# Decay masks from differences of cumulative sums: the broadcast through memory, the subtraction on GpSimd

## The chip, the cores and the metric

The kernel runs on one core of a Trainium2 chip. The metric is the device time of one execution in microseconds (us), median of several runs. The engines are named as the profile names them: PE (TensorE, matmul), DVE (VectorE), ACT (ScalarE), POOL (GpSimd) and SP (SyncE, which only issues DMAs here). Each engine works off its own list of instructions in a fixed order; one that waits for another engine holds up all behind it.

## The reference

A trunk of two layers over a sequence of 256 positions and 2048 features: first a gated delta rule mixer with a convolutional feed-forward block, then a differential attention with another such block. All is float32. The change concerns the mixer's decays alone. Per head (16 of them) the reference has a gate `g` for each position and uses, inside the chunks and between them, exponentials of differences of its cumulative sums:

```python
g = -jnp.exp(a_log) * jax.nn.softplus(a + dt_bias)
...
g = jnp.cumsum(to_chunks(g), axis=-1)
...
decay = jnp.exp(jnp.where(causal, g[..., :, None] - g[..., None, :], -jnp.inf))
...
lower = jnp.where(strict, jnp.einsum('bnhid,bnhjd->bnhij', kb, k) * decay, 0.0)
...
a_intra = jnp.where(causal, jnp.einsum('bnhid,bnhjd->bnhij', q, k) * decay, 0.0)
```

The kernel does not cut the sequence into four chunks. It treats it as two halves of 128 positions, and builds for each head a decay matrix `exp(G_i - G_j)`, zero where i < j, with j on the partitions: one of 128x256 (j in the first half, i in the whole sequence) in the tiles `ma1`, and one of 128x128 (both in the second half) in `ma2`.

## The kernel before

**The weight stream.** Nearly all time goes to products of weights with 2048 features. `wstat` makes one output tile of 128 columns: two transfers of 512 KB bring the weights (`raw`), ACT rounds them to a high part (`hi`, L206), DVE subtracts to get the low part (`lo`, L207), and PE does 16 matmuls with the high part (L228, 128x512) and 16 with the low part (L231, 128x256), all into one PSUM buffer. There are four such buffers (`ps_...`), four each of `raw`, `hi` and `lo`, so a tile's matmuls can't start before the buffer of the tile four places earlier has been read. `add_halves` (L253 and on) reads it: ACT copies one half to a buffer `c_...` (L258; two such buffers exist, tag `c256`), DVE adds the other (L259, which frees the PSUM buffer) and scales by the norm (L261).

**The first layer's opening.** The first three tiles stream together (`ps_in`): the gates (`ba`), the keys of head 0 (`s16`) and its queries (`s0`). Then for each further head a k tile and a q tile follow: k1, q1, k2, q2 and so on. `conv_silu` does the causal convolution of each (ACT L594, DVE L596 three times) and the SiLU (ACT L597, `kq`). `gates_and_decays` is written ahead of the loop over heads. It computes the gates on 16 partitions (L617 to L640, mostly DVE, with an exponential and a logarithm on ACT), transposes them by PE (`bgT_ps`, L644), and builds the decay matrices into the second half of `ma1` and `ma2`. `products` (L567 and on) then makes per head the products of keys with keys and queries on PE (`p1`, `p2`), transposes the queries (L577, squared on ACT, L579, `jq`) and multiplies by the decays on DVE (L583 to L586). The PSUM pool of these small products, `ax`, has four buffers as well.

**What sets the order.** The lists of PE, DVE, ACT and POOL are ordered by a scheduler that simulates the program while it is built; only SP's DMA issues are in the order written. So a change in `gates_and_decays` can move instructions of the k and q tiles around it.

**The decays before.** For four heads at a time DVE multiplies a triangular mask (`upto`) by the gates (L656, 128x512, twice), PE multiplies these by a second mask (`after`) or by ones (L661, L663, L665: `d1`, `d2`, `d3`, fp32, 128x512), which gives the differences of the sums at once in PSUM; DVE copies a column (L667, `sfx`), ACT takes exponentials out of PSUM (L670, L671, and L674 once per head with `sfx` as bias), and POOL zeroes what lies above the diagonal (L676).

Of the kernel before, what the change touches and what calls it, by code (L numbers as in the profile page):

```python
# [8 lines left out]
F32 = mybir.dt.float32  # L9
BF16 = mybir.dt.bfloat16  # L10
F32R = mybir.dt.float32r
AF = mybir.ActivationFunctionType
ALU = mybir.AluOpType
AX = mybir.AxisListType

P = 128
D = 2048
S = 256
KD = D // P
NH = 16  # L20
# [70 lines left out]
class Trunk:  # L91
# [507 lines left out]
    def gates_and_decays(self, ps, ma1, ma2, szt):  # L599
        nc = self.nc  # L600
        s = self.t([P, S], "ba_s", "s256")
        self.add_halves(s[0:64], ps, "ba", slice(0, 64))

        after, upto = szt[0][:, 1024:1152], szt[0][:, 1152:1280]
        nc.gpsimd.affine_select(
            out=after, in_=self.ones, compare_op=ALU.is_gt, fill=0.0,
            base=0, pattern=[[-1, P]], channel_multiplier=1,
        )
        nc.gpsimd.affine_select(
            out=upto, in_=self.ones, compare_op=ALU.is_ge, fill=0.0,  # L610
            base=0, pattern=[[1, P]], channel_multiplier=-1,
# [33 lines left out]
        bgT = self.cst.tile([P, 2, 64], F32, name="bgT")  # L645
        nc.vector.tensor_copy(bgT, pt[:, 0:128].rearrange("p (a c) -> p a c", a=2))


        sfx = self.t([P, NH], "sfx", "sfx", bufs=1)
        for q in range(4):  # L650
            hs = slice(q * 4, (q + 1) * 4)
            gm = []
            for p in range(2):
                o = (q % 2) * 1024 + p * 512
                m = szt[1][:, o:o + 512].rearrange("p (h i) -> p h i", h=4)
                nc.vector.tensor_tensor(  # L656
                    m, upto.unsqueeze(1).to_broadcast([P, 4, P]),
                    bgT[:, p, 32 + q * 4:36 + q * 4].unsqueeze(2).to_broadcast([P, 4, P]), op=ALU.mult)
                gm.append(m)
            d1 = self.ax(f"d1_{q}")  # L660
            nc.tensor.matmul(d1, after, gm[0], start=True, stop=True)  # L661
            d2 = self.ax(f"d2_{q}")
            nc.tensor.matmul(d2, after, gm[1], start=True, stop=True)  # L663
            d3 = self.ax(f"d3_{q}")
            nc.tensor.matmul(d3, self.ones, gm[1], start=True, stop=True)  # L665
            v = lambda x: x.rearrange("p (h i) -> p h i", h=4)
            nc.vector.tensor_copy(sfx[:, hs], v(d1)[:, :, P - 1])  # L667
            m1 = ma1[q].rearrange("p (h a i) -> p h a i", h=4, a=2)[:, :, 1, :]
            m2 = ma2[q // 2].rearrange("p (h a i) -> p h a i", h=8, a=2)[:, (q % 2) * 4:(q % 2) * 4 + 4, 1, :]
            nc.scalar.activation(m1[:, :, 0:P], v(d1), AF.Exp)  # L670
            nc.scalar.activation(m2, v(d2), AF.Exp)  # L671
            for j in range(4):
                h = q * 4 + j
                nc.scalar.activation(m1[:, j, P:S], d3[:, j * P:(j + 1) * P], AF.Exp, bias=sfx[:, h:h + 1])  # L674
            for m in (m1[:, :, 0:P], m2):
                nc.gpsimd.affine_select(out=m, in_=m, compare_op=ALU.is_ge, fill=0.0, base=0, pattern=[[0, 4], [1, P]], channel_multiplier=-1)  # L676
        return bgT[:, :, 0:NH]
# [354 lines left out]
```

## Time and profile before

| | us |
|---|---|
| three runs | 2451.94, 2445.16, 2448.11 |
| median | 2448.11 |
| the profiled execution | 2448.15 |
| its span on the core | 2446.4 |
| PE busy | 2412.2 (99% of the span) |
| DVE busy | 1665.8 (68%) |
| ACT busy | 1194.4 (49%) |
| POOL busy | 115.6 (5%) |
| mean granted clock of PE | 0.993 |

Read it by stage: the shares are means over a span in which nearly all is the weight stream. Times in the trace are from the span's start. The decays belong to the first 100 us: the three first tiles end at about 32, tile k2 starts at 42.65, the gates are done at 68.10, and the d matmuls run between 77.71 and 95.5.

### The profile page before, as it was taken

What the parts mean: (1) busy time and instruction counts of PE and PEld (TensorE: products, weight loads), DVE (VectorE), ACT (ScalarE), POOL (GpSimd) and SP (SyncE); (2) the same over time, 40 slices, a digit from 0 to 9 for tenths busy, and PEclk for the clock granted to TensorE, in tenths of its full rate; (3) what the DMA queues carried; (4) which work ended last, traced back from release to release, by engine and by line L of the source; (5) the groups of instructions that cost most, each with busy time, mean ns of one, the idle gap of its engine ahead of it and who ended that gap; (6) DMA issues with size and microseconds to landing.
All of it is one profiled execution on the core that took longest, in us unless ns stands there. A gap on an engine that the chain in (4) does not pass through costs nothing.

```text
span 2446.4 us, 35043 instructions
## 1 busy us (share of the span) xinstructions
PE 2412.2 (99%) x13211; PEld 2062.6 (84%) x13211; DVE 1665.8 (68%) x2603; ACT 1194.4 (49%) x1956; POOL 115.6 (5%) x185
## 2 busy tenths in 40 slices
PE   9999989999999999999999999999999999999998
PEld 7788868878888888888888888888888888888887
DVE  6888647857877777764446677556777777774444
ACT  6655424545544444444346555445544444444342
POOL 0100730100000000000000000000000000000000
PEclk9999989999999999999999999999999999999999
DMA  6365543444555555565554554455555555555554
GB/s 225 105 201 167 198 142 118 163 160 159 198 189 189 190 189 190 189 207 192 196 192 156 188 188 164 171 187 175 183 189 189 189 190 189 190 195 202 196 193 153
DMA packets 134730, 443.19 MB, mean 181 GB/s; under 512 B 26144, under 2 KB 26400, under 8 KB 134048
## 3 DMA queue, kind: packets, MB, share of 16 engines
q1 hardware_dynamic: 134560, 440.95, 52.9%
q8 instruction: 103, 1.69, 0.3%
q14 instruction: 67, 0.55, 0.1%
HBM read 437.21 MB, written 3.69 MB: 180 GB/s over the span
## 4 chain that ended last, share of the span: by engine, by line
PE 94%; POOL 2%; DVE 1%; ACT 1%; DMA 1%; issue 1%; SPq 0%; DVEq 0%; POOLq 0%; ACTq 0%
PE ps_up L228 26%; PE ps_up L231 13%; PE ps_d L299 7%; PE ps_d L298 7%; PE ps_d L297 7%; PE ps_v L228 3%; PE ps_ak L228 2%; PE ps_aq L228 2%; PE ps_k L228 2%; PE ps_q L228 2%; PE ps_v L231 1%; PE ps_wo L298 1%; PE ps_wo L299 1%; PE ps_av L297 1%; PE ps_av L299 1%; PE ps_av L298 1%
## 5 line engine op out<-in xcount | busy, mean ns | idle before, releaser
L228 PE MATMUL ps_up<-xT_f,hi_up 128*128 128x512 f32 x2752 | 865.7, 396 | 0.0
L231 PEld LDWEIGHTS ps_up<-xT_f,lo_up 128*128 128x128 f32 x2752 | 517.0, 188 | 121.1 <-DVE lo_up L207 0.6
L206 ACT CAST hi_up<-raw_up 128x1024 fp32r<-128x1024 f32 x344 | 360.6, 1050 | 477.7 <-issue 321.0
L207 DVE TENSOR_TENSOR lo_up<-raw_up,hi_up 128x1024 fp32r<-128x1024 f32 x344 | 421.4, 1225 | 198.3 <-ACT hi_up L206 197.9
L231 PE MATMUL ps_up<-xT_f,lo_up 128*128 128x256 f32 x2752 | 541.2, 278 | 0.0
L228 PEld LDWEIGHTS ps_up<-xT_f,hi_up 128*128 128x128 f32 x2752 | 419.3, 189 | 0.2
L207 DVE TENSOR_TENSOR lo_d<-raw_d,hi_d 128x1024 fp32r<-128x1024 f32 x168 | 205.8, 1225 | 224.3 <-ACT hi_d L206 224.3
L206 ACT CAST hi_d<-raw_d 128x1024 fp32r<-128x1024 f32 x168 | 177.0, 1053 | 256.7 <-PE ps_d L299 239.7
L299 PE MATMUL ps_d<-hi_d,hT 128*128 128x512 f32 x672 | 261.8, 390 | 0.0
L298 PE MATMUL ps_d<-lo_d,hT 128*128 128x512 f32 x672 | 261.8, 390 | 0.0
L297 PE MATMUL ps_d<-hi_d,hT 128*128 128x512 f32 x672 | 261.8, 390 | 0.0
L298 PEld LDWEIGHTS ps_d<-lo_d,hT 128*128 128x128 f32 x672 | 126.2, 188 | 26.2
L297 PEld LDWEIGHTS ps_d<-hi_d,hT 128*128 128x128 f32 x672 | 126.2, 188 | 26.2
L299 PEld LDWEIGHTS ps_d<-hi_d,hT 128*128 128x128 f32 x672 | 126.2, 188 | 25.9
L228 PE MATMUL ps_z<-xT_in,hi_z 128*128 128x512 f32 x256 | 82.8, 405 | 9.6 <-ACT hi_z L206 9.6
L228 PE MATMUL ps_v<-xT_in,hi_v 128*128 128x512 f32 x256 | 88.8, 421 | 1.8 <-ACT hi_v L206 1.8
L828 DVE SCALAR_TENSOR_TENSOR gy<-gs,c_fconv,gy 128x255 f32<-128x255 f32 (+1 forms) x176 | 84.3, 480 | 2.9
L228 PE MATMUL ps_ak<-xT_kv,hi_ak 128*128 128x512 f32 x240 | 79.5, 408 | 0.0
L228 PE MATMUL ps_k<-xT_in,hi_k 128*128 128x512 f32 x240 | 77.9, 405 | 1.1 <-DVE s L259 1.1
L228 PE MATMUL ps_q<-xT_in,hi_q 128*128 128x512 f32 x240 | 76.6, 399 | 1.4 <-DVE s L259 1.4
L174 POOL TENSOR_SCALAR qr<-q 128x1 f32<-128x1 f32 x8 | 1.5, 191 | 1584.5 <-DVE q L424 1584.5
L596 DVE SCALAR_TENSOR_TENSOR y<-s,c_gconv,y 128x255 f32<-128x255 f32 (+1 forms) x144 | 68.2, 484 | 9.3 <-ACT y L594 7.6
(382 smaller groups left out, 3890.2 us busy)
## 6 DMA issues: line engine op xcount, KB each, us to landing
raw_up<-in_w_up SPq DMA_DIRECT2D x344, 512.0 KB, 4.3
raw_d<-in_w_dn SPq DMA_DIRECT2D x176, 512.0 KB, 3.3
raw_z<-in_w_in SPq DMA_DIRECT2D x32, 512.0 KB, 3.3
raw_v<-in_w_in SPq DMA_DIRECT2D x32, 512.0 KB, 3.3
raw_wo<-in_w_out SPq DMA_DIRECT2D x32, 512.0 KB, 3.3
raw_av<-in_w_v SPq DMA_DIRECT2D x32, 512.0 KB, 3.2
raw_ao<-in_w_o SPq DMA_DIRECT2D x32, 512.0 KB, 3.3
raw_k<-in_w_in SPq DMA_DIRECT2D x30, 512.0 KB, 3.3
```

The lines of the kernel that those rows point to most:

```text
L174: nc.gpsimd.tensor_scalar(dst, src, scale, EPS, op0=ALU.mult, op1=ALU.add)
L206: nc.scalar.copy(hi[:, c], raw[:, c])
L207: nc.vector.tensor_tensor(lo[:, c], raw[:, c], hi[:, c].bitcast(F32), op=ALU.subtract)
L228: nc.tensor.matmul(to, parts[i][0][:, k % 8 * P:(k % 8 + 1) * P], x, start=(k == 0 and tt != 1), stop=False)
L231: nc.tensor.matmul(ps[i][:, 256:512], parts[i][1][:, k % 8 * P:(k % 8 + 1) * P], xT.hi(k), start=False, stop=(k == KD - 1))
L297: nc.tensor.matmul(ps, xh, hi[:, w], start=(k == 0), stop=False)
L298: nc.tensor.matmul(ps, xh, lo[:, w], start=False, stop=False)
L299: nc.tensor.matmul(ps, xl, hi[:, w], start=False, stop=(k == nk - 1))
L596: nc.vector.scalar_tensor_tensor(y[:, j:S], s[:, 0:S - j], w[:, ct, 3 - j:4 - j], y[:, j:S], op0=ALU.mult, op1=ALU.add)
L828: nc.vector.scalar_tensor_tensor(y[:, j:S], s[:, 0:S - j], w[:, l, f, 2 - j:3 - j], y[:, j:S], op0=ALU.mult, op1=ALU.add)
```

## The change

The masks and the d matmuls go. PE makes the cumulative sums once, as a row per head (`G_row`: three matmuls of 128 columns, after the transposed gates). DVE copies them to `rowS` (32x256, a buffer of tag `c256`), PE transposes that (`G_col`), and DVE negates it (`nG`: -G_j per partition). A DMA on POOL's queue writes `rowS` to memory (`G_d`, 16 KB), and four DMAs of 512 KB, also on POOL's queue, read it back to all 128 partitions into the tiles `szt`. POOL then does per head two `tensor_scalar` (128x256 and 128x128): add -G_j, limit to at most 0. ACT takes the exponential in place, one instruction for the four heads of a `ma1` tile and one for `ma2`, and POOL's masks at the end stay as they were.

```diff
--- before.py
+++ after.py
@@ -601,11 +601,7 @@
         s = self.t([P, S], "ba_s", "s256")
         self.add_halves(s[0:64], ps, "ba", slice(0, 64))
 
-        after, upto = szt[0][:, 1024:1152], szt[0][:, 1152:1280]
-        nc.gpsimd.affine_select(
-            out=after, in_=self.ones, compare_op=ALU.is_gt, fill=0.0,
-            base=0, pattern=[[-1, P]], channel_multiplier=1,
-        )
+        upto = szt[0][:, 1152:1280]
         nc.gpsimd.affine_select(
             out=upto, in_=self.ones, compare_op=ALU.is_ge, fill=0.0,
             base=0, pattern=[[1, P]], channel_multiplier=-1,
@@ -646,32 +642,35 @@
         nc.vector.tensor_copy(bgT, pt[:, 0:128].rearrange("p (a c) -> p a c", a=2))
 
 
-        sfx = self.t([P, NH], "sfx", "sfx", bufs=1)
+
+
+        gs = [bgT[:, p, 32:64] for p in range(2)]
+        row = self.ax("G_row")
+        nc.tensor.matmul(row[0:32, 0:P], gs[0], upto, start=True, stop=True)
+        nc.tensor.matmul(row[0:32, P:S], gs[0], self.ones, start=True, stop=False)
+        nc.tensor.matmul(row[0:32, P:S], gs[1], upto, start=False, stop=True)
+        rowS = self.t([32, S], "G_rowS", "c256")
+        nc.vector.tensor_copy(rowS, row[0:32, 0:S])
+        col = self.ax("G_col")
+        for p in range(2):
+            nc.tensor.transpose(col[:, p * 32:(p + 1) * 32], rowS[:, p * P:(p + 1) * P], self.ident[0:32, 0:32])
+        nG = self.t([P, 64], "nG", "sfx", bufs=1)
+        nc.vector.tensor_scalar(nG, col[:, 0:64], -1.0, None, op0=ALU.mult)
+        gd = self.scr.tile([1, NH * S], F32, name="G_d")
+        nc.gpsimd.dma_start(gd.rearrange("o (h i) -> (o h) i", h=NH), rowS[0:NH])
         for q in range(4):
-            hs = slice(q * 4, (q + 1) * 4)
-            gm = []
-            for p in range(2):
-                o = (q % 2) * 1024 + p * 512
-                m = szt[1][:, o:o + 512].rearrange("p (h i) -> p h i", h=4)
-                nc.vector.tensor_tensor(
-                    m, upto.unsqueeze(1).to_broadcast([P, 4, P]),
-                    bgT[:, p, 32 + q * 4:36 + q * 4].unsqueeze(2).to_broadcast([P, 4, P]), op=ALU.mult)
-                gm.append(m)
-            d1 = self.ax(f"d1_{q}")
-            nc.tensor.matmul(d1, after, gm[0], start=True, stop=True)
-            d2 = self.ax(f"d2_{q}")
-            nc.tensor.matmul(d2, after, gm[1], start=True, stop=True)
-            d3 = self.ax(f"d3_{q}")
-            nc.tensor.matmul(d3, self.ones, gm[1], start=True, stop=True)
-            v = lambda x: x.rearrange("p (h i) -> p h i", h=4)
-            nc.vector.tensor_copy(sfx[:, hs], v(d1)[:, :, P - 1])
+            G = szt[q // 2][:, (q % 2) * 1024:(q % 2 + 1) * 1024]
+            nc.gpsimd.dma_start(G, gd[0:1, q * 1024:(q + 1) * 1024].partition_broadcast(P))
+        for q in range(4):
+            G = szt[q // 2][:, (q % 2) * 1024:(q % 2 + 1) * 1024].rearrange("p (h i) -> p h i", h=4)
             m1 = ma1[q].rearrange("p (h a i) -> p h a i", h=4, a=2)[:, :, 1, :]
             m2 = ma2[q // 2].rearrange("p (h a i) -> p h a i", h=8, a=2)[:, (q % 2) * 4:(q % 2) * 4 + 4, 1, :]
-            nc.scalar.activation(m1[:, :, 0:P], v(d1), AF.Exp)
-            nc.scalar.activation(m2, v(d2), AF.Exp)
             for j in range(4):
                 h = q * 4 + j
-                nc.scalar.activation(m1[:, j, P:S], d3[:, j * P:(j + 1) * P], AF.Exp, bias=sfx[:, h:h + 1])
+                nc.gpsimd.tensor_scalar(m1[:, j, :], G[:, j, :], nG[:, h:h + 1], 0.0, op0=ALU.add, op1=ALU.min)
+                nc.gpsimd.tensor_scalar(m2[:, j, :], G[:, j, P:S], nG[:, 32 + h:33 + h], 0.0, op0=ALU.add, op1=ALU.min)
+            nc.scalar.activation(m1, m1, AF.Exp)
+            nc.scalar.activation(m2, m2, AF.Exp)
             for m in (m1[:, :, 0:P], m2):
                 nc.gpsimd.affine_select(out=m, in_=m, compare_op=ALU.is_ge, fill=0.0, base=0, pattern=[[0, 4], [1, P]], channel_multiplier=-1)
         return bgT[:, :, 0:NH]
```

The line numbers of after are 4 lower from here on (L640 is before's L644), and 1 lower below this function.

On PE the transposes of the gates stood, before, in the third quarter of tile k4 (`ps_k_0_923`; 12 d matmuls stood further down):

```order
L231 MATMUL ps_k_0_923<-xT_in_151,lo_k_0_0_927 128x256 x2
L228 MATMUL ps_k_0_923<-xT_in_170,hi_k_0_1_948 128x512 x2
L231 MATMUL ps_k_0_923<-xT_in_170,lo_k_0_1_949 128x256
L644 MATMUL bgT_ps<-ident,ba_bg 128x64 x2
L231 MATMUL ps_k_0_923<-xT_in_170,lo_k_0_1_949 128x256
```

Now they stand, with the new row and column of sums, between the last matmuls of q1 (`ps_q_0_582`) and the first of k2 (`ps_k_0_656`):

```order
L228 MATMUL ps_q_0_582<-xT_in_189,hi_q_0_1_607 128x512 x2
L231 MATMUL ps_q_0_582<-xT_in_189,lo_q_0_1_608 128x256 x2
L640 MATMUL bgT_ps<-ident,ba_bg 128x64 x2
L649 MATMUL G_row<-sz_391,bgT 32x128
L650 MATMUL G_row<-ones,bgT 32x128
L651 MATMUL G_row<-sz_391,bgT 32x128
L656 MATMUL G_col<-ident,G_rowS 128x32 x2
L228 MATMUL ps_k_0_656<-xT_in_132,hi_k_0_0_659 128x512 x2
```

So the transposes moved up by some four and a half weight tiles (k2, q2, k3, q3 and half of k4), and k2 with all that follows it stands behind them.

On DVE the add that frees the PSUM buffer of the keys of head 0 (`s_508`, L259) stood, before, among the first low parts (`lo`), ahead of all gate work:

```order
L207 TENSOR_TENSOR lo_q_0_1_613<-raw_q_0_1_610,hi_q_0_1_612 128x1024
L259 TENSOR_TENSOR s_508<-ps_in_251,c_qkv_509 128x256
L207 TENSOR_TENSOR lo_k_0_0_665<-raw_k_0_0_662,hi_k_0_0_664 128x1024
L400 COPY rb_in<-rb_in 128x256
L207 TENSOR_TENSOR lo_k_0_1_687<-raw_k_0_1_684,hi_k_0_1_686 128x1024
```

Now that add (`s_503`) is the last row below. The rows above it are the gate chain up to the gates `ba_bg`, and the copies of `bgT` and `G_rowS`, which wait for PE:

```order
L628 TENSOR_SCALAR sz_391<-sz_391 16x256
L629 TENSOR_SCALAR sz_391<-sz_391 16x256
L630 TENSOR_TENSOR sz_391<-sz_391 16x256
L631 TENSOR_TENSOR sz_391<-sz_391 16x256
L632 RECIPROCAL sz_391<-sz_391 16x256
L633 TENSOR_TENSOR sz_391<-sz_391 16x256
L634 TENSOR_TENSOR sz_391<-sz_391 16x256
L635 SCALAR_TENSOR_TENSOR sz_391<-ba_xa,sz_391 16x256
L636 TENSOR_SCALAR ba_bg<-sz_391,ba_nA 16x256
L642 COPY bgT<-bgT_ps 128x128
L653 COPY G_rowS<-G_row 32x256
L259 TENSOR_TENSOR s_503<-ps_in_251,c_qkv_504 128x256
```

In before these gate rows had low parts, adds and convolutions between them; now nothing stands between them, and the add comes behind all. It frees the PSUM buffer that k2 uses.

On ACT a stretch of after, at tile k3's time (`jq_774` is the square of queries for which the next transpose on PE waits):

```order
L594 ACTIVATE y_707<-s_702,c_gconv 128x256
L206 CAST hi_q_0_0_847<-raw_q_0_0_845 128x1024
L672 ACT_TABLE_LOAD
L672 ACTIVATE ma_0_385<-ma_0_385 128x4x256
L579 ACTIVATE jq_646,ssq<-p_0_640 128x128
L673 ACTIVATE ma_0_389<-ma_0_389 128x4x128
L206 CAST hi_q_0_1_869<-raw_q_0_1_867 128x1024
L258 COPY c_qkv_759<-ps_q_0_713 128x256
L597 ACT_TABLE_LOAD
L597 ACTIVATE kq_701<-y_707 128x256
L579 ACTIVATE jq_774,ssq<-p_1_771 128x128
```

The exponential of the decays (L672, L673) now stands as one block for four heads among the casts, with a table load ahead and another behind it. There are 6 table loads before in this stage (one for the logarithm, two for the exponentials, three for SiLU), and 12 now. Ahead of this stretch, the copy of q1's half (`c_qkv1`, L258) takes the `c256` buffer that `rowS` had, and so waits until the DMA to `G_d` has read it. SP's list is the same in both.

## Rows read from the trace of the kernel before

**Rows 1.** The page's fourth part: share of the chain that ended last.

```profile
PE 94%; POOL 2%; DVE 1%; ACT 1%; DMA 1%; issue 1%; SPq 0%; DVEq 0%; POOLq 0%; ACTq 0%
```

**Rows 2.** Timeline, PE, 42 to 80: start, duration, line, out<-in, count [idle before].

```profile
42.65 0.62 PE L228 MATMUL ps_k<-xT_in,hi_k 128*128 128x512 f32 x2
...
48.23 0.63 PE L228 MATMUL ps_q<-xT_in,hi_q 128*128 128x512 f32 x2
...
60.92 0.70 PE L228 MATMUL ps_q<-xT_in,hi_q 128*128 128x512 f32 x2 [1.39 <-DVE s L259]
...
67.87 0.70 PE L228 MATMUL ps_k<-xT_in,hi_k 128*128 128x512 f32 x2 [1.14 <-DVE s L259]
...
71.42 0.34 PE L644 MATMUL bgT_ps<-ident,ba_bg 64*128 64x64 f32 x2
...
78.91 1.02 PE L663 MATMUL d<-sz,sz 128*128 128x512 f32 x2
79.77 1.02 PE L665 MATMUL d<-sz,ones 128*128 128x512 f32 x2
```

**Rows 3.** Timeline, DVE, 36.5 to 100.

```profile
37.01 0.40 DVE L259 TENSOR_TENSOR s<-ps_in,c_qkv 128x256 f32<-128x256 f32 x1
...
46.15 1.22 DVE L207 TENSOR_TENSOR lo_q<-raw_q,hi_q 128x1024 fp32r<-128x1024 f32 x1
...
54.18 0.28 DVE L633 TENSOR_SCALAR sz<-sz 16x256 f32<-16x256 f32 x1
...
56.15 0.41 DVE L634 TENSOR_TENSOR sz<-sz 16x256 f32<-16x256 f32 x1
...
57.44 1.74 DVE L636 RECIPROCAL sz<-sz 16x256 f32<-16x256 f32 x1
...
67.76 0.34 DVE L640 TENSOR_SCALAR ba_bg<-sz,ba_nA 16x256 f32<-16x256 f32 x1
...
71.79 0.29 DVE L646 COPY bgT<-bgT_ps 128x128 f32<-128x128 f32 x1 [0.33 <-PE bgT_ps L644]
```

**Rows 4.** Windows: start:end, length, busy PE, PEld, DVE, ACT, POOL, clock, DMA.

```profile
60.00:70.00 10.00, 7.94 (x44) 6.83 (x45) 9.75 (x17) 4.61 (x7) 0.00 (x0) 1.00 0.57 209
```

**Rows 5.** Timeline, ACT, 36 to 100.

```profile
49.31 1.28 ACT L630 ACT_TABLE_LOAD   x1
50.61 0.42 ACT L630 ACTIVATE sz<-sz 16x256 f32<-16x256 f32 x1
```

**Rows 6.** DMA: the hardware queue, and two issues with their time to landing.

```profile
q1 hardware_dynamic: 134560, 440.95, 52.9%
...
raw_k<-in_w_in SPq DMA_DIRECT2D x30, 512.0 KB, 3.3
...
um_d<-ma SPq DMA_DIRECT2D x32, 16.0 KB, 1.8
```

**Rows 7.** Timeline, POOL, 25 to 330.

```profile
80.58 1.56 POOL L676 TENSOR_SCALAR_AFFINE_SELECT ma<-ma 128x512 f32<-128x512 f32 x2 [47.40 <-ACT ma L670]
...
277.03 0.42 POOL L707 TENSOR_TENSOR pr<-units 128x135 f32<-128x135 f32 x1
277.53 1.33 POOL L710 TENSOR_TENSOR units<-units,pr 128x135 f32<-128x135 f32 x1
...
299.24 0.62 POOL L707 TENSOR_TENSOR pr<-units 128x256 f32<-128x256 f32 x1
299.94 1.60 POOL L710 TENSOR_TENSOR units<-units,pr 128x256 f32<-128x256 f32 x1
```

**Rows 8.** Timeline, DVE, 262 to 272.

```profile
268.01 2.18 DVE L261 TENSOR_TENSOR zs<-zs,rb_in 128x256 f32<-128x256 f32 x1
```

**Rows 9.** Timeline, PE, 325 to 340.

```profile
333.19 1.22 PE L228 MATMUL ps_z<-xT_in,hi_z 128*128 128x512 f32 x2 [9.58 <-ACT hi_z L206]
...
338.89 0.71 PE L228 MATMUL ps_v<-xT_in,hi_v 128*128 128x512 f32 x2
```

**Rows 10.** Windows, from 332.

```profile
332.00:336.00 4.00, 2.77 (x7) 1.86 (x8) 2.05 (x2) 2.36 (x3) 0.00 (x0) 0.50 1.21 185
```


## The prediction

> **What bounds the kernel now.** I read the chain that ended last first: the reader is to see that 94% of it is PE [rows 1]. So a microsecond off PE's list is a microsecond off the time, and work on other engines costs only where PE waits for it. Then PE's timeline over the first 100 us, where the change lies. A weight tile takes 5.58 us (k2 at 42.65, q2 at 48.23), and between 42 and 100 PE waits only twice, 1.39 us ahead of q3 and 1.14 us ahead of k4, both for an add on DVE that frees a PSUM buffer [rows 2]. The reason is in the window of that stage: DVE is busy 9.75 of 10 us there, ACT 4.61, POOL not at all [rows 4]. So DVE is the engine with no room, POOL the one with all of it. All that follows is a sum over these 100 us; I found the lists of instructions alike in the later stages, and carry the sum to the end one to one. Its base is the profiled execution, 2448.15 us with a span of 2446.4; the median of the runs, 2448.11, is the same within 0.04.
>
> **What goes from PE.** Twelve d matmuls (three for each of four groups of heads). Two of them start 0.86 us apart [rows 2], so 12 x 0.86 = 10.3 us, all on PE's list with no wait inside: -10.3. The transposes of the gates leave k4: -0.3 [rows 2]. DVE loses eight masked products, four small copies and the density that makes the two waits; with PE later (below) and DVE lighter I count both as gone: -2.5, between 0 and -2.5.
>
> **What comes in ahead of k2.** This is the largest new term, and the order shows it, not the operations' own cost. PE takes the transposes of the gates right behind q1, so it now waits for the whole gate chain, which before was spread behind four tiles. I follow DVE. Up to the low part that starts at 46.15 [rows 3] it loses five operations like the add of 0.40 at 37.01 [rows 3], 2.0 us in all, of which casts that it waits for take back some: I let that low part start at 44.9 (between 44.2 and 46.15). It ends at 46.1. Then, with nothing between, three scalar operations of 0.28, two tensor operations of 0.41, the reciprocal of 1.74, three more of 0.41 and the last of 0.34 [rows 3]: 0.84 + 0.82 + 1.74 + 1.23 + 0.34 = 4.97, with short steps between them 5.1, so the gates are done at 51.2. The logarithm and its table load, 1.28 + 0.42 [rows 5], run beside the first of these. From the transposes to the start of DVE's copy it was 0.37 (71.42 to 71.79), the copy 0.29 [rows 2, 3]: 51.9. The three row sums have 128 columns each, a quarter of 0.86, so 0.65 with some 0.15 to hand over: 52.7. The copy to `rowS` is like 0.41, and so is the add that frees k2's buffer: 53.6. k2 starts at 53.7 instead of 42.65: +11.0, between +10 and +12.5. All new PE work but the column transposes is inside this number, and those run under the add.
>
> **What the clock takes.** PE would stand idle from 42.7 to about 51.3, 8.6 us, and then do scraps until 53.7. The trace has one such pause: 9.58 us, ended at 333.19 [rows 9], and behind it the granted clock is 0.50, the 1.2 GHz level [rows 10]. From 333.19 to 338.89 PE then did half a tile, 5.70 us for what takes 5.58 / 2 = 2.79 [rows 2, 9]. The two waits of 1.39 and 1.14 lie in a window with clock 1.00 [rows 4]. The new pause is near the long one, so +2.9, between 0 and +3.5.
>
> **ACT.** Each of the four blocks of exponentials is an island between SiLUs, so 12 table loads stand in this stage instead of 6: 6 x 1.28 = 7.7 us more [rows 5], and in return 24 exponentials become 8. ACT has 5.4 of 10 us free [rows 4], so most is hidden. One place is not: in tile k3 the second transpose of head 1's queries waits on PE for a square that stands on ACT behind load, exponential and load. Two loads are 2.6, the exponential of 128x1024 perhaps 1; PE gets there early enough to meet some of it. I take +1.4, between 0 and +3.6.
>
> **The DMAs on POOL's queue.** No row of before shows one: all of its transfers are on the hardware queue [rows 6]. The nearest are 16 KB in 1.8 and 512 KB in 3.3 us to landing [rows 6]. The copy of q1's half on ACT waits until `G_d` has left `rowS`, and behind it stand the convolution and the SiLU of head 0, which `p1_0` needs right behind k2. From 53.2, with 1.8 for the write and some 4.3 for this chain (copy, scaling, convolutions, table load, SiLU), head 0 is ready at about 59.5. k2 at the half clock ends at 53.7 + 5.6 + 2.9 = 62.2. So a landing up to some 4.5 us costs nothing, and each us above it one us. I take 0, with +4 as the other end. The Trainium skill ("DMA: Bandwidth & Descriptors", "Anatomy of one DMA — SWDGE (gpsimd) path") gives about 2.0 us and bytes / 436e3 for such a DMA, by which an estimate is 2.04 us for 16 KB and 3.2 for 512 KB; the sum by that is unchanged, and no row of before can confirm it.
>
> **POOL.** The 32 subtractions have no row. The nearest are its tensor operations of 128x256 and 128x135 late in this layer: 0.62 and 0.42 at their fastest, 1.60 and 1.33 at their slowest [rows 7]. A pair with its gaps is so 1.2 or 3.1 us; a group of four heads 4.8 or 12.4, all of it 19 or 50. `G` is in place at about 59 to 61. At the fast rate the first exponential may start at 64 to 66, about when ACT gets to it, and nothing waits. At the slow rate it is at 71 to 73. DVE pays as well: a product of 128x256 beside POOL took 2.18 where 0.4 is usual [rows 8, 3]. DVE is the engine without room here, so I add +2.5 for its slowing and for late masks, between 0 and +8; the value lies nearer to the fast rows since a mean over alternating fast and slow would be 2.1 a pair, 8.5 a group, and a group is then wanted only every 12 us.
>
> **The sum.** -10.3 - 0.3 - 2.5 + 11.0 + 2.9 + 1.4 + 0 + 2.5 = +4.7, so 2448.15 + 4.7, about 2453.
>
> **The rivals.**
> *A: POOL sets the pace.* If every subtraction takes the slow value, ACT's list stands at its first exponential from about 66 to 72, with casts and squares behind it, and PE stands at the transposes of head 1: about 6 us more than the forecast, 2459. It decides from some 1.4 us per subtraction on: then 8 of them end after 70. For it: both values alternate in the trace, and DVE, the partner, is at 9.75 of 10 [rows 7, 4]. Against: POOL's 128x512 masks beside a busy DVE took 0.78 each (two in 1.56) [rows 7]. The Trainium skill ("SBUF — State Buffer", "SBUF: two separate sides") calls the port pair that both use an exclusive lock, held for a whole instruction against DVE operations with two SBUF inputs. By that rule POOL would wait behind the low parts, 1.22 each, and DVE behind POOL; the spread of rows 7 and the 2.18 of rows 8 agree with it, and the time it gives is this rival's.
> *B: the small write lands late.* Where the queue of POOL needs 7 to 8 us instead of 1.8, `p1_0` waits some 3 us, and the loads behind shift too: 2456. For it: nothing of this kind is in the trace. Against: `um_d` with the same bytes.
> *C: the clock holds and nothing else waits.* Without the 2.9, 1.4 and 2.5 the sum is -2.1: 2446.
> *D: the pause is much shorter.* If k2 started at 48 and not 53.7, with the clock up, it would be -13.1 + 5.4 = -7.7: 2440. For it only that DVE might take the chain sooner; against it the rows of 4.97 us, that can't shrink, and the order, which is fixed.
>
> **How the numbers follow.** What a measurement of this kernel tells from no change is about 0.3%, 7.3 us: 2440.8 to 2455.4. The forecast has 0.46, A 0.28, B 0.12, C 0.10, D 0.04. Faster needs D, 0.05 with its rounding. Slower is A, half of B and about an eighth of the forecast's own spread (2450 to 2457): 0.28 + 0.06 + 0.05 = 0.39. The rest, 0.56, is no difference. The range leaves out D below and the worst of A above (slow POOL and a late write together): 2446 to 2463. The forecast's own is 2450 to 2457.
>
> **What would show it.** In the profile of after: PE idle about 8.6 us ahead of `bgT_ps` and k2 at 53 to 55; a granted clock of 0.5 behind it; no d matmuls, and no wait ahead of q3 and k4; `G_d` landing within 4.5 us; POOL's 128x256 near 0.6 to 1.0. Wrong it would be if k2 starts before 50, if POOL's subtractions are above 1.4, or if PE has waits of several us behind 70 that are put down to ACT's exponentials or to POOL.

## The result: slower, by 0.6%

The changed kernel takes 2465.28 us (median of four runs, 2459.79 to 2466.04), the kernel before 2448.80 beside it: a ratio of 1.0060 (95% interval 1.0048 to 1.0072), and 1.0057 (1.0045 to 1.0070) when it was timed again. I had forecast 2453, in a range up to 2463. The profiled execution has a span of 2462.9, 16.5 us more than before. Its chain of work that ended last has less of PE and more of POOL than [rows 1]:

```profile
PE 91%; POOL 4%; DVE 1%; DMA 1%; ACT 1%; issue 1%; SPq 0%; DVEq 0%; POOLq 0%; ACTq 0%
```

The first place to look is PE from the end of q1 on (its timeline; columns as in [rows 2]):

```profile
53.44 0.47 PE L640 MATMUL bgT_ps<-ident,ba_bg 64*128 64x64 f32 x2 [9.30 <-DVE ba_bg L636]
54.38 0.61 PE L649 MATMUL G_row<-sz,bgT 128*32 128x128 f32 x2 [0.47 <-DVE bgT L642]
...
56.35 0.42 PE L656 MATMUL G_col<-ident,G_rowS 32*128 32x32 f32 x2 [0.51 <-DVE G_rowS L653]
56.90 1.19 PE L228 MATMUL ps_k<-xT_in,hi_k 128*128 128x512 f32 x2
...
64.83 1.02 PE L572 MATMUL p<-kq 128*128 128x512 f32 x2
...
79.09 0.33 PE L577 MATMUL p<-ident,kq 128*128 128x128 f32 x1 [1.55 <-ACT jq L579]
```

```profile
101.83 1.12 PE L572 MATMUL p<-kq 128*128 128x512 f32 x2 [1.58 <-ACT kq L597]
...
116.89 2.07 PE L572 MATMUL p<-kq 128*128 128x512 f32 x2 [2.78 <-ACT kq L597]
```

PE waits 9.30 us for the gates, then k2 starts at 56.90 (before: 42.65 [rows 2]) and lasts to 64.83, 7.93 us where a tile took 5.58. The waits ahead of q3 and k4 are gone, and others have come: 1.55 us for a square, 1.58 and 2.78 for SiLUs of ACT. POOL's 4% in the chain are its subtractions from 65.19 to about 106, one behind the other. That POOL stands there does not say that the others waited for it all that time: ACT's row for the last group of heads has one such wait, and it is short.

```profile
105.78 1.06 ACT L672 ACTIVATE ma<-ma 128x1024 f32<-128x1024 f32 x1 [0.73 <-POOL ma L670]
```

DVE shows the chain that PE waited for:

```profile
46.66 1.15 DVE L207 TENSOR_TENSOR lo_q<-raw_q,hi_q 128x1024 fp32r<-128x1024 f32 x1
...
53.04 0.34 DVE L636 TENSOR_SCALAR ba_bg<-sz,ba_nA 16x256 f32<-16x256 f32 x1
53.95 0.29 DVE L642 COPY bgT<-bgT_ps 128x128 f32<-128x128 f32 x1 [0.57 <-PE bgT_ps L640]
55.88 0.41 DVE L653 COPY G_rowS<-G_row 32x256 f32<-32x256 f32 x1 [1.64 <-PE G_row L651]
56.33 0.42 DVE L259 TENSOR_TENSOR s<-ps_in,c_qkv 128x256 f32<-128x256 f32 x1
```

The low part that I had let start at 44.9 starts at 46.66, the last gate operation at 53.04 (51.2 was forecast as its end), and the add that frees k2's buffer at 56.33. Of this, 1.3 us came ahead of the change's own work: q1 ended at 44.14 in this execution and at 42.81 in that of before (a second execution of the changed kernel, e1 below, has 43.69). That much is scatter: e3, e5 and e9 below, whose lists are the same up to there, have 43.30, 42.90 and 43.21.

The clock behind the pause and the stage in which POOL works (windows, columns as in [rows 4]):

```profile
50.00:60.00 10.00, 5.45 (x19) 4.14 (x20) 6.57 (x14) 1.14 (x3) 0.77 (x1) 0.50 0.06 23
60.00:70.00 10.00, 10.00 (x51) 8.26 (x50) 8.36 (x18) 6.82 (x14) 6.93 (x9) 0.91 0.71 262
...
80.00:90.00 10.00, 10.00 (x60) 8.76 (x59) 7.44 (x12) 8.62 (x14) 10.00 (x8) 1.00 0.46 162
```

The granted clock is 0.50 around the start of k2, as behind the pause of [rows 9, 10]. From 80 to 90 POOL is never idle, PE never either, DVE 7.44 of 10. POOL's new work in groups (count, busy us and mean ns), and the new queue with its issues (KB, median us to landing):

```profile
L670 POOL TENSOR_SCALAR ma<-sz,nG 128x256 f32<-128x256 f32 x16 | 23.2, 1449 | 2.2 <-DVE y L596 2.2
L671 POOL TENSOR_SCALAR ma<-sz,nG 128x128 f32<-128x128 f32 x16 | 15.8, 989 | 0.0
...
L675 POOL TENSOR_SCALAR_AFFINE_SELECT ma<-ma 128x512 f32<-128x512 f32 x8 | 6.9, 884 | 0.0
```

```profile
q0 software_dynamic: 608, 2.11, 0.2%
...
sz<-G_d POOLq DMA_DIRECT2D x4, 512.0 KB, 5.4
...
G_d<-G_rowS POOLq DMA_DIRECT2D x1, 16.0 KB, 3.7
```

So a subtraction took 1.45 or 0.99 us, near the slow rows of [rows 7]; the write to memory landed in 3.7 us (1.9 to 3.7 in the experiments below that have it) against 1.8 for the same bytes on the hardware queue [rows 6], the broadcasts in 5.4 against 3.3.

Where the 16.5 us arose can be told by the start of a few tiles. These are PE's rows for the tile `ps_z` in before and after (duration min/median/max in ns, then first and last start in us):

```profile
L228 PE MATMUL ps_z<-xT_in,hi_z x256: 390/397/796, 235.2 to 338.0; 128*128 128x512 f32 x128
```

```profile
L228 PE MATMUL ps_z<-xT_in,hi_z x256: 390/396/796, 246.5 to 351.1; 128*128 128x512 f32 x128
```

The table has the first of these starts for all kernels, the time from it to the end of the long pause (in before 333.19, [rows 9]), and from there to the first matmul of `ps_wo`; the experiments e1 to e18 are told below. The ratios compare all runs of a kernel; the other columns are one profiled execution each, up to 3.8 us from its kernel's median.

| kernel | ratio to before (95%) | first z tile at | to the end of the long pause | to the first wo tile |
|---|---|---|---|---|
| before | 1 | 235.2 | 98.0 | 142.1 |
| before, second execution (e8) | - | 235.2 | 99.7 | 141.9 |
| after | 1.0060 (1.0048 to 1.0072) | 246.5 | 99.8 | 145.2 |
| after, again (e1) | 1.0057 (1.0045 to 1.0070) | 244.5 | 99.2 | 144.2 |
| e2 written late | 1.0022 (1.0013 to 1.0031) | 237.0 | 100.8 | 142.8 |
| e3 no subtraction | 1.0063 (1.0051 to 1.0076) | 244.2 | 100.3 | 145.1 |
| e4 before without d | 0.9995 (0.9986 to 1.0004) | 231.0 | 99.6 | 145.2 |
| e5 after, v order of before | 1.0047 (1.0034 to 1.0060) | 246.5 | 99.8 | 144.2 |
| e6 before, v order of after | 1.0005 (0.9996 to 1.0013) | 234.9 | 99.5 | 144.0 |
| e7 without d, v order of before | 0.9979 (0.9971 to 0.9988) | 231.6 | 99.0 | 143.6 |
| e9 pause filled | 1.0027 (1.0016 to 1.0038) | 242.5 | 100.4 | 144.3 |
| e10 inside head 0 | 1.0020 (1.0011 to 1.0029) | 236.2 | 99.6 | 142.8 |
| e11 the same, ACT's bias | 1.0007 (0.9998 to 1.0016) | 235.6 | 98.5 | 143.9 |
| e12 the same, on DVE | 1.0010 (1.0001 to 1.0019) | 236.6 | 101.2 | 143.9 |
| e13 no d, no exponentials | 0.9981 (0.9972 to 0.9989) | 231.0 | 98.7 | 141.7 |
| e14 no d, no masked products | 0.9986 (0.9977 to 0.9995) | 232.8 | 98.5 | 143.6 |
| e15 no decays | 0.9991 (0.9983 to 1.0000) | 230.7 | 100.3 | 142.3 |
| e16 shared | 0.9998 (0.9989 to 1.0007) | 231.5 | 100.2 | 147.2 |
| e17 shared, v order of before | 0.9994 (0.9985 to 1.0003) | 232.1 | 100.3 | 143.5 |
| e18 no gates, no decays | 0.9947 (0.9934 to 0.9961) | 222.8 | 99.4 | 143.1 |

From the first wo tile to the end all take 1970 to 1974. Of the 16.5 us, 11.3 are there at the first z tile (9.3 in the second execution), 1.8 arise up to the pause's end, where before itself scatters by 1.7, and 3.1 in the v stage.

### The profile page after: what moved, and what is told of

It is laid out like the page before. It is cut to its first block, busy times and chain, and to the rows that moved or that the text cites. A ratio compares the mean times of both kernels' runs of the same rounds, so it can differ in the third digit from the quotient of the medians.

```text
span 2462.9 us, 35016 instructions
## 1 busy us (share of the span) xinstructions
PE 2411.2 (98%) x13195; PEld 2063.0 (84%) x13195; DVE 1667.1 (68%) x2593; ACT 1200.5 (49%) x1946; POOL 162.3 (7%) x221
## 4 chain that ended last, share of the span: by engine, by line
PE 91%; POOL 4%; DVE 1%; DMA 1%; ACT 1%; issue 1%; SPq 0%; DVEq 0%; POOLq 0%; ACTq 0%
PE ps_up L228 26%; PE ps_up L231 13%; PE ps_d L298 6%; PE ps_d L297 6%; PE ps_d L299 6%; PE ps_v L228 3%; PE ps_ak L228 2%; PE ps_aq L228 2%; PE ps_k L228 2%; PE ps_q L228 2%; PE ps_v L231 1%; PE ps_wo L298 1%; PE ps_wo L299 1%; PE ps_wo L297 1%; PE ps_av L299 1%; PE ps_av L298 1%
## 5 line engine op out<-in xcount | busy, mean ns | idle before, releaser
L596 DVE SCALAR_TENSOR_TENSOR y<-s,c_gconv,y 128x255 f32<-128x255 f32 (+1 forms) x144 | 71.3, 497 | 12.9 <-ACT y L594 10.9
```

What stands on the lines that cost most here:

```text
L596: nc.vector.scalar_tensor_tensor(y[:, j:S], s[:, 0:S - j], w[:, ct, 3 - j:4 - j], y[:, j:S], op0=ALU.mult, op1=ALU.add)
```

## The experiments

**What the order costs (e1, e2).** e1 is the changed kernel once more. e2 moves nothing but the place in the program:

```diff
-        beta = self.gates_and_decays(gate, ma1, ma2, szt)   # with the row sums and all behind them
+        bgT, upto = self.gates_and_decays(gate, ma1, ma2, szt)
...
             self.conv_silu(kq[:, 1, :], qk[1], h)
+            if h == 1:
+                self.decays(bgT, upto, ma1, ma2, szt)
```

> The changed kernel once more, unchanged. Theory 1 (the order of the lists makes the loss: the gate chain stands whole ahead of tile k2): again 14 to 17 us over before, with the pause of about 9 us ahead of the gates' transposes and half clock behind it. Open point: from the first z tile to the first wo tile the profiled execution took 245.0 us against 240.1 before. If that belongs to the change, 244 to 246 again; if it is the scatter of one execution, any value between 240 and 245.

> The same instructions as the changed kernel, but the part from the row sums on is written behind the convolutions of head 1 in the program, so that the gate chain spreads between the low parts as before and the transposes stand behind tile q3. Theory 1 (the order): no pause ahead of k2, no half clock, the d matmuls' 10.3 us come out: 2438 to 2446. Theory 2 (POOL's subtractions and ACT's blocks of exponentials hold PE): still 2455 or more, with waits for the squares and SiLUs.

e1 repeats the result, but leaves open what it was to settle: from the first z to the first wo tile it takes 243.4 us, between the 240.1 of before and the 245.0 of the changed kernel, and just under the 244 that would have put the difference down to the change. e2 gives back 8 to 9 us of it (1.0022 instead of 1.0057), but not the gain that theory 1 wanted: by its 2455.32 it falls on theory 2's edge. PE's waits of e2 from 36 to 240:

```profile
PE p L577 <- DVE ma L589: 2.0, 1, 2.0
PE ps_q L228 <- DVE s L259: 1.4, 1, 1.4
PE G_col L663 <- DVE G_rowS L660: 1.3, 1, 1.3
PE bgT_ps L643 <- DVE ba_bg L639: 1.1, 1, 1.1
```

The pause of 9.3 us is gone and the clock holds at k2. In its place stand 2.9 us at the transposes and row sums, with a clock of 0.83 on the mean from 60 to 80, and some 3 us later. The clock falls here without a long pause, behind waits of 1.10, 0.47 and 1.33 us with only small matmuls between them:

```profile
70.00:80.00 10.00, 8.66 (x28) 5.56 (x27) 9.64 (x26) 4.47 (x12) 3.62 (x6) 0.66 0.60 217
```

Hardly a wait is for ACT's squares or SiLUs, as theory 2 wanted (0.4 in all). So the place in the program is most of the loss, and something else keeps the d matmuls' time.

**POOL's part (e3).**

```diff
-                nc.gpsimd.tensor_scalar(m1[:, j, :], G[:, j, :], nG[:, h:h + 1], 0.0, op0=ALU.add, op1=ALU.min)
...
+                nc.scalar.activation(m1[:, j, :], G[:, j, :], AF.Exp, bias=nG[:, h:h + 1])
```

> POOL does no subtraction: it masks the broadcast sums in place (8 masks as before), and ACT takes the exponential per head with the negated column as its bias (32 instructions instead of 8). The gate chain still stands ahead of k2. Theory 1: the pause and the half clock stay, only the waits behind 70 shrink: 2455 to 2463. Theory 2: 2444 to 2451.

Neither: 1.0063, as slow as the changed kernel. The waits:

```profile
PE bgT_ps L640 <- DVE ba_bg L636: 9.4, 1, 9.4
PE p L572 <- ACT kq L597: 4.4, 2, 3.1
...
PE p L577 <- ACT jq L579: 0.5, 1, 0.5
```

```profile
76.95 1.74 PE L572 MATMUL p<-kq 128*128 128x512 f32 x2 [3.08 <-ACT kq L597]
...
98.27 1.12 PE L572 MATMUL p<-kq 128*128 128x512 f32 x2 [1.36 <-ACT kq L597]
```

```profile
60.00:70.00 10.00, 10.00 (x55) 8.35 (x55) 9.42 (x18) 9.91 (x16) 4.75 (x6) 0.99 0.74 256
70.00:80.00 10.00, 6.92 (x30) 4.87 (x29) 2.34 (x5) 9.93 (x21) 5.40 (x5) 0.87 0.15 52
```

There are again 4.4 us for SiLUs without a single subtraction on POOL, but they are other waits: 3.08 and 1.36 at 76.95 and 98.27 here, 1.58 and 2.78 at 101.83 and 116.89 in the changed kernel. In e3 ACT does 32 exponentials instead of 8 and is full, 9.9 of 10 us from 60 to 80. So e3 moved the work to an engine that then held PE up, and does not tell what the subtractions cost on POOL in the changed kernel.

**What the d matmuls were worth (e4).** The exponentials read the masked products, and the sums are left out:

```diff
-            d1 = self.ax(f"d1_{q}")
-            nc.tensor.matmul(d1, after, gm[0], start=True, stop=True)
...
+            d1, d2 = gm
+            d3 = gm[1].rearrange("p h i -> p (h i)")
```

> The kernel before without its twelve d matmuls: the exponentials read the masked products directly, so the sums are left out of the computation. Theory 1: the full price of the matmuls comes off, 10.3 us and up to 2.5 of the two waits: 2435 to 2440. Rival: DVE is full in this stage and turns part of it into waits: 2441 to 2447.

Both were wrong: 0.9995, no gain that can be told (with the v order of before, e7 below, 0.9979 or 5 us, in which 2441 to 2447 would have been right). Here is the one new wait, and the stage around it:

```profile
87.04 1.66 PE L572 MATMUL p<-kq 128*128 128x512 f32 x2 [3.92 <-ACT kq L597]
```

```profile
80.00:120.00 40.00, 36.08 (x187) 29.38 (x187) 37.80 (x98) 30.32 (x72) 8.43 (x9) 0.96 0.44 137
```

Of 10.3 us, 3.9 come back as a wait for a SiLU, and the clock falls behind it (mean 0.96 over these 40 us). The SiLU is late because ACT works without a gap from 73.75 to 87.04, with 24 exponentials, two table loads and casts. ACT was as full in before, from 80 to 90; it is the window of [rows 4], 60 to 70, that shows it half free. First before, then e4:

```profile
80.00:90.00 10.00, 10.00 (x41) 6.35 (x39) 8.22 (x17) 9.94 (x22) 2.83 (x4) 1.00 0.32 118
```

```profile
80.00:90.00 10.00, 6.08 (x26) 4.49 (x26) 9.86 (x25) 9.94 (x24) 7.66 (x8) 0.87 0.33 105
```

DVE is busy 37.8 of 40 us from 80 to 120, against 30 before: PE comes earlier to the heads, and more of their work on DVE falls into this stretch. At the first z tile 4.2 us are left, and the stage from the pause to the first wo tile takes 145.2 instead of 142.

**The v stage (e5, e6, e7, e8).** That stage has the same instructions in all these kernels. But the lists of PE differ there: e4's is word for word that of the changed kernel, and not that of before. The scheduler, simulating, arrives at the v tiles at another time, and places the heads' pieces differently. A few idle matmuls behind z tile 12, where PE waits for POOL later anyway, set the one order or the other, or nearly it (12 for e5 and e7, 4 for e6), with all lists up to tile z1 unchanged. Of PE's 850 instructions in that stage e5 has 756 and e7 822 at the place of before, and e6 826 of 854 at that of the changed kernel:

```diff
+                if h == 12:
+                    dj = self.ax("dj")
+                    for _ in range(12):
+                        nc.tensor.matmul(dj[:, 0:P], self.ones, self.ones, start=True, stop=True)
```

> The changed kernel with 12 idle matmuls (128 columns, 0.2 us each) written behind z tile 12, where PE later waits for POOL anyway. All lists up to tile z1 are those of the changed kernel word for word, but the scheduler now puts the v tiles and the heads in the order of the kernel before. Theory A (the other order of the v stage costs some 3 us): 2460 to 2462. Theory B (the longer z and v stages are scatter of single executions): 2463 to 2466.

> The kernel before with 4 such matmuls: its lists up to tile z1 unchanged, its v stage in the order of the changed kernel. Theory A: 2451 to 2453. Theory B: 2447.5 to 2450.

> The kernel before without its d matmuls (the sums are left out of the computation) with 12 such matmuls, which give its v stage the order of the kernel before. Theory A: 2444.5 to 2446.5, so a part of the 10.3 us appears. Theory B: 2447.5 to 2450 as in the run without the idle matmuls.

> The kernel before once more, for a second profiled execution: Theory A: from the first z tile to the first wo tile 239 to 242 us again, the pause ahead of the last z tile 9 to 11. Theory B: anything up to 245.

The medians point one way: e5 is 0.10% below e1 and e6 0.05% above before, each within the intervals, and e7 0.16% below e4, where the intervals only just touch. In the table the stage to the first wo tile takes 141.7 to 144.3 with the order of before or nearly it, and 144.0 to 145.2 with that of the changed kernel. But one and the same list scatters as much: before, e9, e12 and e18 share PE's list in that stage and take 141.9 to 144.3, e11 and e16 share another and take 143.9 and 147.2. So the medians lean to A, and that the order costs the 3.1 us is not shown. e8 fits A by its 141.9, though its pause was 11.27 us; its 99.7 shows that the 98.0 to the pause's end in the first execution was a good one.

**The pause (e9).** 18 idle matmuls stand on PE between q1 and the gates' transposes:

```diff
+        dj = self.ax("dj")
+        for _ in range(18):
+            nc.tensor.matmul(dj[0:64, 0:256], self.ones[0:64, 0:64], s[0:64, 0:256], start=True, stop=True)
         pt = self.ax("bgT_ps")
```

> The changed kernel with 18 idle matmuls (64x64x256, about 0.43 us each) on PE between q1 and the gates' transposes, so that PE waits some 1 to 2 us there instead of 9; its v stage has the order of before, so it compares with the run that had the changed kernel with that order (2460.5, ratio 1.0047). If the pause costs by the clock too: the granted clock stays up behind it and tile k2 takes 5.6 us instead of 7.9, 2457 to 2459. If the clock's loss is hidden by later waits: 2459.5 to 2461.5.

The time fell by more than expected (2455.07; 1.0027 for 1.0047), yet not in the way that I meant:

```profile
43.14 7.98 PE L640 MATMUL dj<-ba_s,ones 64*64 64x256 f32 x36
52.62 0.34 PE L643 MATMUL bgT_ps<-ident,ba_bg 64*128 64x64 f32 x2 [1.50 <-DVE ba_bg L636]
...
55.85 1.22 PE L228 MATMUL ps_k<-xT_in,hi_k 128*128 128x512 f32 x2
...
63.53 1.02 PE L572 MATMUL p<-kq 128*128 128x512 f32 x2
```

```profile
50.00:60.00 10.00, 7.48 (x29) 5.35 (x28) 7.29 (x19) 2.50 (x6) 2.64 (x5) 0.67 0.05 16
```

PE was busy for 8 us, to 51.12, and the clock fell all the same, but not at once: it is 1.00 from 52 to 53, 0.71 from 53 to 54 and 0.50 from 54 on, behind waits of 1.50, 0.47 and 0.51 us with small matmuls between them. e2 shows such a fall with no idle matmuls and no pause ahead, so e9 doesn't tell whether the idle matmuls counted. k2 took 7.68 us. What became less are the later waits (5.1 us for 5.8 in e5) and the dips of the clock behind them, of which e5 has two and e9 none up to z. The profiled execution took 2458.91, one of two near 2459 among seven; the other five took 2454 to 2456, and no trace shows their clock. So the price of the clock at k2 stays 2.1 to 2.4 us as measured, and why the median fell stays open.

**Other places and engines for the decays (e10, e11, e12).** All three write the decays inside the products of head 0, behind its matmuls, and have the v order of before (e12) or nearly it (e10, e11). e10 leaves the work as it is, e11 is e10 with e3's edit, e12 puts the subtractions on DVE:

```diff
+        if between:
+            between()          # the decays, for head 0
         nc.vector.tensor_tensor(m1[:, 0, :], p1[:, 0:256], m1[:, 1, :], op=ALU.mult)
...
-                nc.gpsimd.tensor_scalar(m1[:, j, :], G[:, j, :], nG[:, h:h + 1], 0.0, op0=ALU.add, op1=ALU.min)
+                nc.vector.tensor_scalar(m1[:, j, :], G[:, j, :], nG[:, h:h + 1], 0.0, op0=ALU.add, op1=ALU.min)
```

> The changed kernel with the part from the row sums on written inside the products of head 0, behind their matmuls, so that PE has its products of head 0 ahead of the row sums; v stage as before. If the remaining loss of the late version was the 2.9 us of waits at the row sums and the clock behind them: 2448 to 2451. If it is that ACT and DVE are full between 60 and 130 us: 2452 to 2457 again.

> As the last one, but without subtractions on POOL: it masks the sums in place, ACT takes the exponential per head with the column as bias. If POOL's 1.2 us per subtraction and the late masks hold the heads: 2443 to 2448, faster than before. If ACT is the one that is full: 2449 to 2455.

> As the run before the last, but with the 32 subtractions on DVE instead of POOL. If DVE is full in this stage, its 32 operations (0.2 to 0.4 us each, about 9 us) cost most of that: 2453 to 2460. If POOL held the heads more than that: 2445 to 2450.

e10 (1.0020) is 0.27% below e5, which has the same work and a v order that is likewise near that of before: 6.6 us, the cleanest price of the early place. Against e2 (1.0022) it wins nothing: the clock holds and the waits at the row sums shrink from 2.9 to 1.3 us, but 4.2 us of waits for squares stand in their place. e11 (1.0007) and e12 (1.0010) come out near before, e12's interval just above 1. They are 3.0 and 2.7 us faster than e10, timed beside them, and differ from it by where the subtractions are made (e11 also in some of the v stage's order): in this place POOL's subtractions cost about that. e12 lies between its two forecasts, and PE then waits for DVE once:

```profile
PE ps_q L231 <- DVE lo_q L207: 7.0, 1, 7.0
```

```profile
77.94 0.35 DVE L677 TENSOR_SCALAR ma<-sz,nG 128x256 f32<-128x256 f32 x1 [1.14 <-DMA sz<-G_d]
78.21 0.28 DVE L678 TENSOR_SCALAR ma<-sz,nG 128x128 f32<-128x128 f32 x1
...
84.20 1.99 DVE L678 TENSOR_SCALAR ma<-sz,nG 128x128 f32<-128x128 f32 x1
...
86.25 1.91 DVE L678 TENSOR_SCALAR ma<-sz,nG 128x128 f32<-128x128 f32 x1
```

```profile
82.02 1.92 POOL L682 TENSOR_SCALAR_AFFINE_SELECT ma<-ma 128x512 f32<-128x512 f32 x2 [6.11 <-ACT ma L679]
83.89 4.19 POOL L700 MEMSET t<- 128x2048 f32 x2
```

The same subtraction takes 0.28 us while POOL is idle and up to 1.99 while POOL sets memory. The low part that PE waits for stands behind 24 such subtractions, 81.65 to 93.33 with one other low part; by their fast steps they would take some 5.5 us (an estimate from the rows above), so about half of the 11.7 us is the stretch beside POOL.

**The ceiling (e13, e14, e15, e18).** These leave out, on e7's base, ACT's exponentials (e13), DVE's masked products (e14), both (e15), and both with the gate chain (e18). The decays, and in e18 the gates, are constants then.

```diff
-            nc.scalar.activation(m1[:, :, 0:P], v(d1), AF.Exp)       # e13, e15, e18
...
-                nc.vector.tensor_tensor(                              # e14, e15, e18
-                    m, upto.unsqueeze(1).to_broadcast([P, 4, P]),
...
-        nc.vector.reciprocal(bg[B], bg[B])                            # e18, with all of L617 to L640
```

> On the kernel before without d matmuls and with before's v order (run above: ratio 0.9979, with a wait of 3.9 us for a SiLU of ACT and half clock behind it), ACT's 24 exponentials of the decays are left out as well (the tiles hold a constant, so the decays are left out of the computation). If ACT was what kept the d matmuls' 10.3 us from showing: no such wait, ratio 0.9945 to 0.9962. If it was DVE: about 0.998 again.

> On the same base DVE's eight masked products (0.7 us each) and four copies are left out instead, so that the exponentials read a constant (the decays are left out of the computation). If DVE kept the gain back: 0.9945 to 0.9962. If ACT: about 0.998 with a wait of 3 us or more for ACT.

> Both left out with the d matmuls: no decays at all, the v order of before. The most that any way of making decays can win: if PE's time is then the bound, 0.9940 to 0.9958 (10.3 us, the 2.5 us of waits and little more); if DVE and ACT bound this stage by the weight stream's own work, 0.996 to 0.998.

> As the run without any decays, and the gate chain itself is left out too (constants instead of the gates; v order of before). That takes some 9 us of small operations from DVE between 41 and 68. If DVE bounds the stage up to the d matmuls: PE's waits of 6.4 us for the add on DVE shrink to 3 or less and the ratio falls to 0.9955 to 0.9975. If DVE is not what holds it: 0.998 to 1.000, with waits as long.

e13 and e14 win no more than e7 (PE waits 4.2 and 4.3 us there for one add on DVE, where e7 and before have 1.4), and e15, which makes no decays at all, 0.1%. They are no clean ceiling: POOL writes the constants in the opening, ahead of its part of the norm, and the norm's scale reaches DVE at 43.3 to 47.7 instead of 38.5 (e13, e14, e15, e18). In e13, e14 and e15 DVE is 9.7 to 9.8 of 10 us busy from 60 to 70, where PE comes to wait; how much of that is the late norm is not known. PE's waits of e15, then windows of e15 and of e18 (e18 has no wait at all in that stretch):

```profile
PE ps_q L228 <- DVE s L259: 6.4, 2, 3.4
```

```profile
40.00:80.00 40.00, 33.62 (x181) 28.33 (x180) 34.12 (x64) 21.80 (x37) 0.00 (x0) 0.96 0.49 156
```

```profile
40.00:80.00 40.00, 39.92 (x223) 33.45 (x222) 34.88 (x79) 23.81 (x46) 0.00 (x0) 1.00 0.55 182
```

With the gate chain PE is busy 33.62 of 40 us and waits 6.4 for adds on DVE, 3.4 of it at 52.11 behind the late norm; without the chain PE is full though the norm is as late, the first z tile starts at 222.8, and the time falls by 0.53%, 11.5 us between the medians and more than forecast. 235.2 - 222.8 = 12.4 is close to what I had taken off: 10.3 + 2.5. So the d matmuls' time can be had when DVE is rid of the gate operations that stand among the low parts, 8 us by their durations. Whether that is needed is not shown: no run leaves out the gate chain alone, or the decays without the late norm.

**A version that might win (e16, e17).** Heads 0 to 7 as in e11, heads 8 to 15 as in e10; e17 adds 8 idle matmuls for the v order.

```diff
+            if q < 2:      # masked sums, exponential per head with the column as bias
...
+            else:          # subtraction on POOL, one exponential per tile
```

> A version of the change that might beat both: decays written inside head 0's products, heads 0 to 7 by ACT with the column as bias, heads 8 to 15 by POOL's subtraction and one exponential per tile. If the halves relieve each other: 2442 to 2448. If waits of ACT and POOL only change places: 2449 to 2455.

> The shared version with 8 idle matmuls behind z tile 12, which give its v stage the order of the kernel before; its lists up to the z tiles are those of the shared version, whose first z tile started at 231.5 (before: 235.2) and whose stage from the pause to the first wo tile took 147.2 (before: 142). If the v stage's order took that gain back: 2444 to 2447, faster than before. If not: 2448 to 2450.

Both fall at the edge of what was expected or just beside it. e17 is 16 us better than the changed kernel and 0.06% below before, inside its interval: no version with the whole computation beats the kernel before clearly.

## Why the prediction was wrong

The mechanism ahead of k2 was right, and so was its place. What failed is the first step, "a microsecond off PE's list is a microsecond off the time", and with it the -10.3 and -2.5. Taken off alone, this work leaves 4.2 us (e4) or 3.6 us (e7) at the first z tile and 1 to 5 us in the time: ACT, which I had read as 5.4 of 10 us free, is full where PE then comes to the heads.

- **The d matmuls, -10.3, and the two waits, -2.5.** They are off PE's list, but little of it reaches the time: e4 takes them off alone and the kernel is 0.05% faster, e7 0.21%. What takes it back in e4 is the wait of 3.9 us for ACT and the clock behind it. I had read ACT's 4.61 of 10 in one window [rows 4]; twenty microseconds on, where the heads' products begin, it is 9.94. I had also read DVE's 9.75 of 10 there and drawn from it only that POOL had room. That DVE holds this stage, too, is argued: the two waits of before are for DVE, and e18, rid of the gate chain, has the 12.4 us; but the runs that leave out the decays with the chain in place (e13 to e15) have the late norm on DVE as well.
- **The place ahead of k2, +11.0.** Measured: 14.25 late, less 1.3 that q1 was late already, 12.9. Of the 1.9 us too much, 0.5 came up to the low part (46.66 for 44.9, less the 1.3), 0.4 in the chain, which also waited 0.48 for the logarithm, and 1.0 behind it, where the row sums ran at half clock, 0.40 to 0.43 us from one to the next.
- **The clock, +2.9.** 2.35 at k2 (7.93 - 5.58), and a second dip of some 1.7 near 120 in one of two executions.
- **ACT, +1.4.** The wait at head 1's square was 1.55. I had not seen the two waits for SiLUs, 4.4 us. e4 has a like wait, 3.9, with nothing but the d matmuls gone, so they may be PE's freed time coming back; that is argued, not shown for these two. Waits of several us behind 70 for ACT were one of my signs of being wrong; 1.55, 1.58 and 2.78 us are such waits.
- **POOL and contention, +2.5.** Not separated in the changed kernel, as e3 loads ACT; in the later place 2.7 to 3.0 us (e10 against e12 and e11), near the 2.5, in part by luck as the place is another. Rival A had its condition fulfilled (1.45 us a subtraction, my other sign of being wrong) and its time nearly, 2459, but its mechanism shows only in 0.73 us that ACT waited for POOL. The Trainium skill ("SBUF — State Buffer", "SBUF: two separate sides") says that a DVE operation of certain kinds and a POOL operation lock each other out of a shared port pair for a whole instruction. e12's 0.28 against 1.91 and 1.99 us, the long ones ending with POOL's two memsets, agrees; what it costs the changed kernel is not shown.
- **The DMAs, 0.** Right in its effect: 3.7 us for the write is within the 4.5 that I gave it, and p1 of head 0 did not wait.
- **"I found the lists of instructions alike in the later stages."** They are not in the v stage. I had taken pieces moved by a tile or two for no difference, and so carried the sum to the end one to one; the profiled executions are 3.1 us apart there. That the order is the cause is not shown, as one list scatters by 2 to 3 us.

The sum of the profiled execution: 12.9 + 1.3 + 2.35 + 1.7 + 1.55 + 4.4 + 0.2 (a second, short wait for a square) - 13.1 = 11.3 up to the z tiles, as the table has it. Here the -13.1 stands in full, and the waits for ACT and the second dip of the clock take back some 7.9 of it. Then 1.8 up to the pause's end, no more than before differs from itself (98.0 and 99.7), and 3.1 in the v stage, and 0.3 to the end.

What stays open: why e9's idle matmuls shortened the later waits, whether the order of the v stage has a cost beyond its scatter, what POOL's subtractions cost in the early place, and whether DVE's gate chain alone holds back the d matmuls' time.

## To carry to other kernels

Before you take work off the leading engine, read each other engine's share over the whole stretch that will move up, not in one window: ACT was at 4.61 of 10 in one and at 9.94 twenty microseconds on, and there the leading engine came to wait for it. A run with the work left out tells how much is to be had, if what stands in its place costs nothing elsewhere: here the constants held up the opening. And a substitute that moves work to another engine does not price the first: e3 took the subtractions off POOL and filled ACT. Where a scheduler orders the lists by a simulation, an edit's place in the program can cost more than its instructions; moving the same code behind the work that it must not hold up won 6.6 us. Compare the lists of the later stages as well, and where they differ, time one list more than once before you lay a few us to the order.

## What the runs showed of the hardware that was not expected

- The granted clock fell to 0.50, the 1.2 GHz level, not only behind a pause of 9.3 us, but also behind three short waits with only small matmuls between: 1.10, 0.47 and 1.33 us in e2 (0.66 from 70 to 80), and 1.50, 0.47 and 0.51 in e9, behind 8 us of idle fp32 matmuls (0.67 from 50 to 60). The 1.39 and 1.14 of before, with whole tiles between, lie at 1.00. Whether the idle matmuls counted is not shown.
- A broadcast DMA of 512 KB from POOL's queue landed in 5.4 us (median of four on the way together; 5.2 to 5.8 in the experiments) where loads of the same size on the hardware queue took 3.3, and 16 KB in 1.9 to 3.7 against 1.8. The estimate by the Trainium skill ("DMA: Bandwidth & Descriptors", "Anatomy of one DMA — SWDGE (gpsimd) path"), 2.04 and 3.2 us, was nearly met for 16 KB in e3 and e9 (1.9), too low by up to 1.7 elsewhere, and too low by 2.2 for 512 KB; no run has one alone.
- POOL's `tensor_scalar` with a column as operand took 1.45 us on the mean for 128x256 beside a DVE that was busy 7 to 9 of 10 us; DVE did the same in 0.35 with POOL idle (e12).
